# Two projection stages whose later attention outputs are loaded by channel block and split once

## Chip, cores and metric

The kernel runs on one core of a Trainium2 chip. The metric is the device time of one execution in microseconds (us); lower is better. A "TensorE clock" below is the clock that the chip granted, as a share of 2.4 GHz: 1.00 is 2.4 GHz, 0.50 is 1.2 GHz.

## What is computed

Two token groups (prompt and sample), each 1024 tokens by 1024 channels, go through the same two layers. The first layer is attention, the second a pooling mixer.

```python
for l in range(2):
    shift, scl, gate = split(silu(c) @ ada_w[l] + ada_b[l])
    h = rmsnorm(x, pre_norm[l]) * (1 + scl) + shift
    m = attn_mixer(h) if l == 0 else pool_mixer(h)
    x = x + gate * rmsnorm(m, post_norm[l])

def attn_mixer(h):                 # y @ w_out is the "projection" of this study
    qa, ka, va, qb, kb, vb, gate = split(h @ w_in)
    oa = dilated_window_attention(rope(qa), rope(ka), va)           # 8 heads of 64
    ob = grouped_query_attention(axial_rope(rmsnorm(qb, gq)),
                                 axial_rope(rmsnorm(kb, gk)), vb)   # 8 heads, 2 kv heads
    y = concat(oa, ob) * silu(gate)
    return y @ w_out
```

All matrix products are in fp32 accuracy: each operand is split into a rounded part (`hi`, fp32r) and the remainder (`lo`), and three products hi·hi, hi·lo and lo·hi are summed in PSUM.

## The kernel before

The program runs, in this order: prompt attention, prompt projection (stage s = 0), sample attention, sample projection (stage s = 1), sample pooling layer, prompt pooling layer. A planner orders each engine's instructions ahead of time from its own estimate of durations; what it orders, each engine and the DMA queue of SyncE ("SP" in the rows) then run strictly in that order. `keep_in_program_order` (`pin`) keeps an instruction in the order in which the code names it. `issue_after(ins)` keeps the instructions traced under it behind `ins` on the engine of `ins`. Tile pools give out SBUF space; a tile that takes over the space of an older one waits until the older one has been read for the last time.

**A projection stage** (`outproj0`) walks over 8 tiles of 128 tokens. For each tile TensorE sums 8 channel blocks, 6 matmuls of 512 columns each, into one PSUM tile `S` (`out_mm`, L1012 to L1014); there are two `S` tiles, so tile i + 2 may start when tile i has been read. Reading it is ScalarE's square (`square`, L1165) and VectorE's multiplication (L1166); then VectorE adds the row of x (`added`, L1168), and SyncE stores it (`x1o`, L1169). For s = 1 the row is normalised right away (`normed`: ScalarE L250, VectorE L255 and L256) and turned by TensorE (L268) into the next layer's input, two tiles later. For s = 0 the stage makes the sample attention's input from normalised rows kept in DRAM (`h_affine`, L341 to L343).

The left operand y comes from DRAM, where the attention heads stored it as (channel, token). Tiles 0 to 3 were loaded and split during the attention (`out_pre`), and the products of tiles 0 and 1 are almost done when the stage starts. For tiles 4 to 7 the stage loads y tile by tile: two loads of 256 KB for one tile, each 128 partitions by 4 channel blocks by 128 tokens, so in runs of 512 bytes (`load_y`, L1094). The loads of tile i + 2 stand in SyncE's queue in pinned order behind the store of tile i - 1 and the load of row i + 2, which itself waits for a free one of four row buffers. The split of tile i + 1 (ScalarE L1100, VectorE L1101, two of each) is traced in the middle of tile i's matmuls (`split_y`).

**Behind stage s = 0** the sample attention starts with its key and value unit (`unit_KV`): four pairs of 128-token tiles, 48 matmuls of 256 columns each (L416 to L418), copied out by ScalarE, normalised and rotated on VectorE and GpSimd with the table `tb` of k (`b_norm`), split (`hl`, L574 and L575), and turned by TensorE (L437). Then follows the first query unit (`unit_P`), whose weights come from two tiles `raw` and are split by VectorE and GpSimd (L351, L352). The tables of q and k are made by `consts_B` at the start of that attention: three loads (L383, L387), nine VectorE instructions (L388 to L399).

**In the sample pooling layer**, while its third output product (`outp`) runs, `h_affine` makes the prompt layer's input (L341 to L343) between the gate (`gate_ct`, L1257) and the sum `m` (L1320), all on VectorE.

Of the kernel before, what the change touches and what calls it, by code (L numbers as in the profile page):

```python
# [13 lines left out]
P = 128  # L14
D = 1024
# [45 lines left out]
class Trunk:  # L61
# [256 lines left out]
    def h_affine(self, pool, tags, ahead, hT, src, col, gp):  # L318
# [13 lines left out]
        for k in range(KT):  # L332
            if not behind:
                load()
# [45 lines left out]
    def consts_B(self, ap, bp):  # L380
        nc, t = self.nc, self.t
        cs = ap.tile([P, 2, NT, 32], F32, name=self.n("ropB0"), tag="X", bufs=1)
        nc.sync.dma_start(cs, t["k_ropB"])  # L383
        self.ropB = {}
        gt = ap.tile([P, 3, HD], F32, name=self.n("g0"), tag="r2", bufs=2)
        for i, nm in enumerate(("gq", "gk")):
            nc.sync.dma_start(gt[:, i], t[nm].to_broadcast([P, HD]))  # L387
        nc.vector.tensor_scalar_mul(gt[:, 2], gt[:, 0], 0.125)  # L388
        for nm, g in (("gq", gt[:, 2]), ("gk", gt[:, 1])):
            if nm == "gq":  # L390
                tb = bp.tile([P, 2, NT, HD], F32, name=self.n("tb"), tag="s4", bufs=1)
            else:
                tb = ap.tile([P, 2, NT, HD], F32, name=self.n("tb"), tag="P", bufs=3)
            gl = g[:, None, 0:32].to_broadcast([P, NT, 32])
            gh = g[:, None, 32:64].to_broadcast([P, NT, 32])
            nc.vector.tensor_tensor(tb[:, 0, :, 0:32], cs[:, 0], gl, ALU.mult)
            nc.vector.tensor_tensor(tb[:, 0, :, 32:64], cs[:, 0], gh, ALU.mult)
            nc.vector.scalar_tensor_tensor(tb[:, 1, :, 0:32], cs[:, 1], -1.0, gh, op0=ALU.mult, op1=ALU.mult)
            nc.vector.tensor_tensor(tb[:, 1, :, 32:64], cs[:, 1], gl, ALU.mult)  # L399
            self.ropB[nm] = tb  # L400
# [138 lines left out]
    def unit_KV(self, ap, subs, hT, out):  # L539
# [19 lines left out]
        todo = []  # L559
        for pr in range(4):  # L560
# [10 lines left out]
            for h in range(2):  # L571
                hl = ap.tile([P, 2, 4, HD], F32R, name=self.n("hl"), tag="rhl", bufs=2)
                kb = x[:, :, h : h + 1, :].to_broadcast([P, 2, 2, HD])
                nc.vector.tensor_copy(hl[:, :, 0:2, :], kb)  # L574
                nc.vector.tensor_tensor(hl[:, :, 2:4, :], kb, hl[:, :, 0:2, :].bitcast(F32), ALU.subtract)  # L575
                todo.append((pr, h, hl))
            for h in range(2):
# [56 lines left out]
    def layer0(self, s, hT, ap, side, after_proj, open2, run_h, first=None):  # L634
# [4 lines left out]
        if s == 1:  # L639
            self.consts_B(ap, ap)  # L640
# [57 lines left out]
        next(gens[2])  # L698
# [363 lines left out]
    def outproj0(self, s, wo, op, hN, pre):  # L1062
# [4 lines left out]
        yv = self.y_d[s].rearrange("(k p) c -> p k c", p=P)  # L1067
        hq, late = [], []
        y0, yh, xt, jk, hx, ws = {}, {}, {}, {}, {}, []
# [9 lines left out]
        def load(i):  # L1079
            return nc.sync.dma_start(new(i, xt, "xt", 4), xsrc[i])  # L1080

        def new_y(i):
            if i not in yh:
                yh[i] = [tile([P, 2, 4, P], F32R, "yh", 4) for f in range(2)]

        def new_y0(i):
            if i not in y0:
                y0[i] = [tile([P, 4, P], F32, "y0", 4) for f in range(2)]

        def load_y(i):  # L1090
            if 4 <= i < NT:
                new_y0(i)
                for f in range(2):
                    pin(nc.sync.dma_start(y0[i][f], yv[:, 4 * f : 4 * f + 4, i * P : (i + 1) * P]))  # L1094

        def split_y(i):
            if 4 <= i < NT:
                new_y(i)
                for y, z in zip(yh[i], y0[i]):
                    nc.scalar.activation(y[:, 0], z, AF.Copy)  # L1100
                    nc.vector.tensor_tensor(y[:, 1], z, y[:, 0].bitcast(F32), ALU.subtract)  # L1101
# [10 lines left out]
        def new_ws():  # L1112
            ws.extend(tile([P, 2, 256], F32, "ws", 4) for _ in range(4))

        hN_of = perm = g1 = sh1 = None
        if s == 0:
            for i in range(3):
                load(i)
            pg = self.mrow(op, 0, s, 2, "pg")
            new(0, jk, "jk", 2)  # L1120
            hN_of = self.h_affine(op, (("xk", 4),), 4, hN, self.xn_d, self.col[:, 1], ())
            load_k = next(hN_of)
            new_y(4)
            new_y0(4)
            new_ws()
        else:
            new(0, jk, "jk", 2)
            new_y(4)
            new(0, hx, "hx", 2)
            g1, sh1 = (self.row(op, x) for x in ("g1", "sh1"))  # L1130
            new_ws()
            new_y0(4)
# [5 lines left out]
            nc.sync.dma_start(perm, t["k_perm"])  # L1138
            self.mrow(op, 1, s, 1, None, g1)
            self.mrow(op, 1, s, 0, None, sh1)  # L1140
        ks = (0, 1, 1, 2, 1, 2, 1, 0)
        src = t["pwin"][0] if s else t["win"][8]
        for i in range(NT):
            load_y(i + 2)
            if i == 4:
                self.wi = 1
                self.kvw = self.base.tile([P, 2, KT, 256], F32R, name=self.n("w"), tag="w", bufs=1)
                for q in range(4):
                    pin(nc.sync.dma_start(ws[q], src[:, 2 * q : 2 * q + 2, :]))
            if i < 2:  # L1150
                ps = pre[0][i]
            else:
                ps = self.ptile("S")
                for k in range(KT):
                    y, q = (pre[1][i], k) if i < 4 else (yh[i][k // 4], k % 4)
                    self.out_mm(ps, y, q, wo, k, k == 0, k == KT - 1)
                    if k % 2 == 1:
                        run_h(1)
                    if k == 3:
                        split_y(i + 1)  # L1160
            hq += late
            j = new(i, jk, "jk", 2)
# [7 lines left out]
            if i + 3 < NT:  # L1170
                pin(load(i + 3))
# [502 lines left out]
```

## Time and profile before

| | |
|---|---|
| median of 3 runs | 2333.75 us (2332.66 to 2338.61) |
| the profiled execution | 2335.37 us, with a span of 2333.5 us and 1.9 us around it |
| mean granted TensorE clock | 0.965 |
| stage s = 0, tiles 2 to 7 | 822.3 to 902.2 us |
| stage s = 1, tiles 2 to 7 | 1613.6 to 1729.7 us |

The profile is that of one execution. A window row gives, for a stretch of time, each engine's busy time with its number of instructions, then the granted TensorE clock and the DMA engines' share and rate. A wait row says which instruction waited, for whom, for how long in total, how often, and the longest. Matmuls overlap, so busy time of TensorE hides a lower clock: the clock column shows it.

### The profile page before, as it was taken

What the parts mean: (1) busy time and instruction counts of PE and PEld (TensorE: products, weight loads), DVE (VectorE), ACT (ScalarE), POOL (GpSimd) and SP (SyncE); (2) the same over time, 40 slices, a digit from 0 to 9 for tenths busy, and PEclk for the clock granted to TensorE, in tenths of its full rate; (3) what the DMA queues carried; (4) which work ended last, traced back from release to release, by engine and by line L of the source; (5) the groups of instructions that cost most, each with busy time, mean ns of one, the idle gap of its engine ahead of it and who ended that gap; (6) DMA issues with size and microseconds to landing.
All of it is one profiled execution on the core that took longest, in us unless ns stands there. A gap on an engine that the chain in (4) does not pass through costs nothing.

```text
span 2333.5 us, 38514 instructions
## 1 busy us (share of the span) xinstructions
PE 2140.1 (92%) x13777; PEld 1900.1 (81%) x13777; DVE 1572.6 (67%) x3465; ACT 1065.9 (46%) x2435; POOL 979.5 (42%) x1421
## 2 busy tenths in 40 slices
PE   6999899999999788999999999978689999999998
PEld 4987788899999667998897999967467888788887
DVE  8788888777777744778877776784345544874546
ACT  6455555666666421456666666653222112211112
POOL 3676665123543402643311353442024345673452
PEclk8999999999999799999999999989889999999999
DMA  6123343111212453100000221133233223241113
GB/s 254 54 85 116 98 121 100 47 43 52 67 55 60 139 163 116 37 24 27 25 25 28 62 66 57 46 108 116 88 95 95 95 82 126 83 166 41 59 42 148
DMA packets 162784, 193.26 MB, mean 83 GB/s; under 512 B 16184, under 2 KB 126112, under 8 KB 162592
## 3 DMA queue, kind: packets, MB, share of 16 engines
q1 hardware_dynamic: 162288, 190.01, 25.9%
q8 instruction: 109, 1.79, 0.3%
q10 hardware_dynamic: 304, 0.79, 0.1%
q14 instruction: 83, 0.68, 0.1%
HBM read 148.56 MB, written 42.18 MB: 82 GB/s over the span
## 4 chain that ended last, share of the span: by engine, by line
PE 34%; DVE 11%; DMA 6%; ACT 4%; POOL 3%; issue 3%; SPq 0%; POOLq 0%; DVEq 0%; ACTq 0%
PE S L1199 3%; PE S L1200 3%; PE S L1201 3%; DMA y<-y_d 3%; PE J L416 2%; PE J L417 2%; PE J L418 2%; PE S L1296 2%; PE S L1297 2%; PE S L1298 2%; PE H L743 2%; PE T L781 2%; DVE E L761 1%; POOL w L352 1%; DVE w L351 1%
## 5 line engine op out<-in xcount | busy, mean ns | idle before, releaser
L352 POOL TENSOR_TENSOR w<-ws,w 128x256 fp32r<-128x256 f32 (+1 forms) x410 | 387.5, 959 | 314.5 <-DVE w L351 229.8
L416 PE MATMUL J<-w,hT 128*128 128x256 f32 x1664 | 481.8, 290 | 2.8 <-ACT xj L429 2.1
L417 PE MATMUL J<-w,hT 128*128 128x256 f32 x1664 | 478.2, 287 | 3.0 <-POOL w L352 2.8
L418 PE MATMUL J<-w,hT 128*128 128x256 f32 x1664 | 477.0, 287 | 3.6 <-DVE hT L1445 3.4
L416 PEld LDWEIGHTS J<-w,hT 128*128 128x128 f32 x1664 | 318.5, 191 | 7.1 <-ACT xj L429 3.9
L417 PEld LDWEIGHTS J<-w,hT 128*128 128x128 f32 x1664 | 318.5, 191 | 7.1 <-POOL w L352 5.2
L418 PEld LDWEIGHTS J<-w,hT 128*128 128x128 f32 x1664 | 318.0, 191 | 6.3 <-DVE hT L1445 4.1
L761 DVE TENSOR_TENSOR E<-T,E 128x512 fp32r<-128x512 f32 x384 | 261.9, 683 | 83.4 <-ACT E L760 80.8
L760 ACT ACTIVATE E<-T 128x512 fp32r<-128x512 f32 x384 | 226.7, 598 | 198.0 <-PE T L781 70.3
L351 DVE CAST w<-ws 128x256 fp32r<-128x256 f32 (+1 forms) x412 | 181.7, 465 | 152.1 <-PE S L1201 72.0
L750 ACT ACTIVATE P<-H,mx 128x512 f32<-128x512 f32 x256 | 173.9, 686 | 109.3 <-DVE mx L745 92.8
L1199 PE MATMUL S<-hT,w 128*128 128x512 f32 x512 | 200.6, 392 | 3.2 <-DVE sg L1257 2.9
L1200 PE MATMUL S<-hT,w 128*128 128x512 f32 x512 | 200.4, 391 | 0.0
L1201 PE MATMUL S<-hT,w 128*128 128x512 f32 x512 | 200.1, 391 | 0.0
L744 DVE TENSOR_REDUCE mx<-H 128x1 f32<-128x512 f32 x256 | 173.7, 682 | 32.5 <-PE H L743 30.8
L781 PE MATMUL T<-identr,P 128*128 128x128 f32 x1024 | 163.6, 275 | 3.7 <-DVE E L761 3.1
L794 PE MATMUL O<-E,v 128*128 128x256 f32 x512 | 143.9, 303 | 15.2 <-DVE E L761 14.5
L860 ACT ACTIVATE P<-H,nm 128x256 f32<-128x256 f32 x256 | 117.9, 474 | 80.3 <-DVE nm L854 79.8
L793 PE MATMUL O<-E,v 128*128 128x256 f32 x512 | 147.2, 296 | 5.2 <-DVE X L815 2.8
L781 PEld LDWEIGHTS T<-identr,P 128*128 128x128 f32 x1024 | 123.5, 141 | 19.5 <-DVE E L761 2.1
L502 POOL TENSOR_TENSOR hl<-xj,hl 128x256 fp32r<-128x256 f32 x64 | 48.3, 758 | 210.1 <-DVE hl L501 141.7
L125 POOL TENSOR_SCALAR rv<-ss 128x1 f32<-128x1 f32 x64 | 22.1, 345 | 254.7 <-ACT hx L1165 78.7
(271 smaller groups left out, 5255.9 us busy)
## 6 DMA issues: line engine op xcount, KB each, us to landing
ws<-win SPq DMA_DIRECT2D x184, 128.0 KB
ws<-ada_w SPq DMA_DIRECT2D x128, 128.0 KB
ws<-pwin SPq DMA_DIRECT2D x64, 256.0 KB
vb<-v_d SPq DMA_DIRECT2D x64, 144.0 KB
xt<-xp SPq DMA_DIRECT2D x16, 512.0 KB
ada<-ada_w SPq DMA_DIRECT2D x16, 512.0 KB
v_d<-v SPq DMA_DIRECT2D x64, 128.0 KB
wos<-wout SPq DMA_DIRECT2D x32, 256.0 KB
```

What stands on the lines that cost most here:

```text
L351: nc.vector.tensor_copy(hi, src)
L352: (nc.vector if dve_lo else nc.gpsimd).tensor_tensor(lo, src, hi.bitcast(F32), ALU.subtract)
L416: nc.tensor.matmul(ps, hi, w[:, 0, k, :], start=(k == 0), stop=False)
L417: nc.tensor.matmul(ps, hi, w[:, 1, k, :], start=False, stop=False)
L418: nc.tensor.matmul(ps, lo, w[:, 0, k, :], start=False, stop=(k == KT - 1))
L750: nc.scalar.activation(p[:, c * 512 : (c + 1) * 512], ps[c], AF.Exp, bias=mx[:, 2:3], accum_out=stat[h][:, i, c : c + 1])
L760: nc.scalar.activation(ov[0], Tv, AF.Copy)
L761: nc.vector.tensor_tensor(ov[1], Tv, ov[0].bitcast(F32), ALU.subtract)
L781: nc.tensor.transpose(T[:, (2 * e + i) * P : (2 * e + i + 1) * P], Pt[(h, 2 * g + i)][:, (2 * kp + e) * P : (2 * kp + e + 1) * P], self.ident)
L1199: nc.tensor.matmul(ps[:, cs], w[:, 0, k, ws], hT[:, k, 0, cs], start=(k == 0), stop=False)
L1200: nc.tensor.matmul(ps[:, cs], w[:, 0, k, ws], hT[:, k, 1, cs], start=False, stop=False)
L1201: nc.tensor.matmul(ps[:, cs], w[:, 1, k, ws], hT[:, k, 0, cs], start=False, stop=(k == KT - 1))
```

## The change

Five parts.

1. In both stages y of tiles 4 to 7 is loaded by channel block: eight loads of 128 channels by the last 512 tokens (256 KB, runs of 2 KB), four of them ahead of the tile loop, the other four as the four buffers `y0` come free. Each block is split once, 512 columns, into a tile `yk` that stays for the stage. Blocks 0 to 2 (in the order 0, 1, 2, 4, 5, 6, 7, 3) are split behind tile 0's `square` and `added`, three more behind tile 1's, the last two behind tile 2's. The matmuls of tiles 4 to 7 take the blocks in that order.
2. To make room there are three row buffers `xt` in place of four, loaded two tiles ahead, three `xk` in place of four, one `jk` for s = 1, and the staged weights `ws` use the `y0` buffers.
3. For s = 0 the loads of the next attention's table constants are issued in the stage at tile 5, and the tables are made behind the last tile's `added` (`table_B`, `tab_q`).
4. `kvd` lists the last split of k (L575) of each pair in `unit_KV`. With it, the rounding of the `raw` weights in `unit_P` is put behind the first pair's last split of k, and the loading and rounding of the second query unit's weights behind the third pair's.
5. In the sample pooling layer each step of `h_affine` is put behind the gate and the sum `m` of the tile before.

```diff
-    def consts_B(self, ap, bp):
+    def consts_B(self, cs, gt, pin=lambda x: x):
...
+        pin(nc.sync.dma_start(cs, t["k_ropB"]))
...
+            pin(nc.sync.dma_start(gt[:, i], t[nm].to_broadcast([P, HD])))
+
+    def table_B(self, nm, tb):
...
     def unit_KV(self, ap, subs, hT, out):
...
+            self.kvd.append(x_)
...
     def unit_P(self, ap, subs, hT, i, out):
-        w = self.load_block(ap, self.t["win"][9 + i], i == 0, raw=raw, z=2 if raw else 1)
+        with self.tc.issue_after(self.kvd[0].ins) if raw else ExitStack():
+            w = self.load_block(ap, self.t["win"][9 + i], i == 0, raw=raw, z=2 if raw else 1)
...
     def layer0(self, s, hT, ap, side, after_proj, open2, run_h, first=None):
...
         if s == 1:
-            self.consts_B(ap, ap)
+            with self.tc.issue_after(self.last.ins):
+                self.table_B("gk", ap.tile([P, 2, NT, HD], F32, name=self.n("tb"), tag="P", bufs=3))
+                self.tab_q(ap)
...
-        next(gens[2])
+        with self.tc.issue_after(self.kvd[2].ins):
+            next(gens[2])
...
     def outproj0(self, s, wo, op, hN, pre):
...
-    pin(nc.sync.dma_start(y0[i][f], yv[:, 4 * f : 4 * f + 4, i * P : (i + 1) * P]))
+        def load_y(k):
+            if k not in y0:
+                y0[k] = tile([P, 512], F32, "y0", 4)
+            return nc.sync.dma_start(y0[k], self.y_d[s, k * P : (k + 1) * P, 512:])
+
+        def split_y(k, behind):
+            if k not in yk:
+                yk[k] = tile([P, 2, 512], F32R, "yk", 8)
+            with ExitStack() as es:
+                for ins in behind:
+                    es.enter_context(self.tc.issue_after(ins.ins))
+                nc.scalar.activation(yk[k][:, 0], y0[k], AF.Copy)
+                nc.vector.tensor_tensor(yk[k][:, 1], y0[k], yk[k][:, 0].bitcast(F32), ALU.subtract)
...
+        order = (0, 1, 2, 4, 5, 6, 7, 3)
...
+            for k in order[:4]:
+                load_y(k)
...
+        ky = ((0, 1, 2), (3, 4, 5), (6, 7))
...
-            if i + 3 < NT:
-                pin(load(i + 3))
+            if 0 < i < NT - 2:
+                pin(load(i + 2))
...
+            if i < 3:
+                for n in ky[i]:
+                    split_y(order[n], (square, added))
+                    if n + 4 < KT:
+                        load_y(order[n + 4])
...
+            if s == 0 and i == 5:
+                cg = tile([P, D], F32, "xk", 3)
+                self.consts_B(cg[:, 0:512].rearrange("p (a t d) -> p a t d", a=2, t=NT),
+                              cg[:, 512 : 512 + 3 * HD].rearrange("p (a d) -> p a d", a=3), pin)
+            self.last = added
...
     def layer1(self, s, hT, lp, hp, run_h, open_l2):
...
-                outp(prev, False, False, each=lambda i: next(h_of))
+                outp(prev, False, False, each=lambda i: i and h_of.send((self.lastg, self.lastm)))
+                h_of.send((self.lastg, self.lastm))
```

## Rows read from the trace of the kernel before

**Rows 1.** The page's first part: busy time, share and instructions of each engine.
```profile
PE 2140.1 (92%) x13777; PEld 1900.1 (81%) x13777; DVE 1572.6 (67%) x3465; ACT 1065.9 (46%) x2435; POOL 979.5 (42%) x1421
```

**Rows 2.** Windows by stage: engines' busy time, PEclk, DMA share, GB/s.
```profile
822.30:844.40 22.10, 22.04 (x96) 17.93 (x96) 8.64 (x8) 3.06 (x4) 1.30 (x3) 1.00 0.47 167
844.40:902.20 57.80, 47.11 (x193) 37.84 (x194) 28.84 (x30) 15.62 (x22) 7.84 (x10) 0.91 0.46 152
902.20:968.70 66.50, 54.16 (x426) 53.21 (x425) 36.23 (x80) 16.21 (x45) 33.92 (x50) 0.90 0.22 68
1613.60:1638.10 24.50, 24.41 (x112) 19.57 (x112) 9.74 (x9) 4.28 (x8) 3.25 (x6) 1.00 0.28 97
1638.10:1729.70 91.60, 61.55 (x226) 47.30 (x227) 37.44 (x42) 20.67 (x38) 14.77 (x25) 0.80 0.25 77
1972.00:2057.00 85.00, 79.33 (x331) 63.81 (x330) 65.23 (x57) 22.76 (x29) 53.67 (x41) 0.96 0.39 139
```

**Rows 3.** Waits of TensorE from 844 to 969 us.
```profile
PE T L437 <- DVE hl L574: 10.4, 1, 10.4
PE S L1012 <- ACT yh L1100: 9.9, 1, 9.9
PE J L417 <- POOL w L352: 1.9, 2, 1.6
```

**Rows 4.** Waits of TensorE from 1638 to 1730 us.
```profile
PE S L1012 <- DVE jk L1166: 22.9, 4, 7.8
PE T L268 <- DVE hx L256: 7.3, 4, 2.5
```

**Rows 5.** Chain that ended last, in stage s = 1: start, duration, what.
```profile
1614.97 10.79 DMA x_d<-xt
...
1627.16 15.64 DMA y<-y_d
1642.83 0.63 ACT yh L1100
1643.46 1.01 ACT hx L1165 x2
1644.49 1.24 DVE jk L1166
```

**Rows 6.** Timeline of ScalarE and VectorE: the split of y, one half tile.
```profile
853.52 0.63 ACT L1100 ACTIVATE yh<-y 128x512 fp32r<-128x512 f32 x1 [17.77 <-DMA y<-y_d]
854.18 0.69 DVE L1101 TENSOR_TENSOR yh<-y,yh 128x512 fp32r<-128x512 f32 x1 [16.20 <-ACT yh L1100]
```

**Rows 7.** The same chain earlier: a weight load of 256 KB in runs of 2 KB.
```profile
1549.95 4.31 DMA wos<-wout
```

**Rows 8.** Timeline of SyncE's queue as the two stages begin.
```profile
820.79 1.27 SPq L327 DMA_DIRECT2D xk<-xn_d  x3
1599.55 2.04 SPq L244 DMA_DIRECT2D row<-mod_d  x2
```

**Rows 9.** The chain from the end of stage s = 0 to the key unit.
```profile
904.13 9.71 DMA g<-gk
...
914.61 1.29 DVE xt L1168
915.91 10.43 DMA x_d<-xt
...
926.47 2.51 DVE w L351 x4
...
932.05 0.19 POOL rv L125
...
936.34 0.30 DVE hl L574
```

**Rows 10.** Window in which the key unit's matmuls run without a wait.
```profile
912.00:926.00 14.00, 14.00 (x121) 14.00 (x120) 4.16 (x10) 2.41 (x7) 0.00 (x0) 1.00 0.36 113
```

**Rows 11.** Wait of TensorE from 1972 to 2057 us, sample pooling layer.
```profile
PE S L1296 <- DVE m L1320: 3.8, 1, 3.8
```

More of the change, by code (lines that the diff above doesn't have):

```diff
@@ L332, in h_affine @@
         for k in range(KT):
-            if not behind:
+            if ahead:
                 load()
@@ L1079, in load @@
         def load(i):
[L1080 to L1093, printed above, removed]
-                    pin(nc.sync.dma_start(y0[i][f], yv[:, 4 * f : 4 * f + 4, i * P : (i + 1) * P]))
[L1096 to L1101, printed above, removed]
+            return nc.sync.dma_start(new(i, xt, "xt", 3), xsrc[i])
+        def load_y(k):
[10 more added lines that the diff above has]
+                nc.vector.tensor_tensor(yk[k][:, 1], y0[k], yk[k][:, 0].bitcast(F32), ALU.subtract)
         def run_h(c):
@@ L1110, in run_h @@
                         hq.pop(0)
-        def new_ws():
-            ws.extend(tile([P, 2, 256], F32, "ws", 4) for _ in range(4))
+        order = (0, 1, 2, 4, 5, 6, 7, 3)
         hN_of = perm = g1 = sh1 = None
         if s == 0:
+            pg = self.mrow(op, 0, s, 2, "pg")
             for i in range(3):
                 load(i)
-            pg = self.mrow(op, 0, s, 2, "pg")
-            new(0, jk, "jk", 2)
[L1121 to L1125, printed above, removed]
-        else:
-            new(0, jk, "jk", 2)
-            new_y(4)
+            hN_of = self.h_affine(op, (("xk", 3),), 0, hN, self.xn_d, self.col[:, 1], ())
+            load_k = next(hN_of)
+            load_k()
+            for k in order[:4]:
+                load_y(k)
+            new(0, jk, "jk", 2)
+        else:
+            new(0, jk, "jk", 1)
+            for k in order:
+                yk[k] = tile([P, 2, 512], F32R, "yk", 8)
             new(0, hx, "hx", 2)
             g1, sh1 = (self.row(op, x) for x in ("g1", "sh1"))
-            new_ws()
-            new_y0(4)
+            y0[0] = tile([P, 512], F32, "y0", 4)
             load(0)
@@ L1148, in outproj0 @@
                 for q in range(4):
+                    ws.append(tile([P, 2, 256], F32, "y0", 4))
                     pin(nc.sync.dma_start(ws[q], src[:, 2 * q : 2 * q + 2, :]))
@@ L1153, in outproj0 @@
                 ps = self.ptile("S")
-                for k in range(KT):
-                    y, q = (pre[1][i], k) if i < 4 else (yh[i][k // 4], k % 4)
-                    self.out_mm(ps, y, q, wo, k, k == 0, k == KT - 1)
+                for k in range(KT) if i < 4 else order:
+                    if i < 4:
+                        y, q = pre[1][i], k
+                    else:
+                        y, q = yk[k][:, :, (i - 4) * P : (i - 3) * P].rearrange("p e (q c) -> p e q c", q=1), 0
+                    self.out_mm(ps, y, q, wo, k, k == 0, k == (KT - 1 if i < 4 else order[-1]))
                     if k % 2 == 1:
                         run_h(1)
-                    if k == 3:
-                        split_y(i + 1)
             hq += late
-            j = new(i, jk, "jk", 2)
+            j = new(i, jk, "jk", 1 if s else 2)
             h = new(i, hx, "hx", 2) if s else j
@@ L1319, in outp @@
                 else:
[L1320 removed]
+                    self.lastm = nc.vector.tensor_tensor(mi, ps, mi, ALU.add)
                 if last:
@@ L1448, in start @@
             load_x(i, "qT", 4)
-        self.consts_B(ap, ap)
+        self.consts_B(ap.tile([P, 2, NT, 32], F32, name="ropB0", tag="X", bufs=1),
+                      ap.tile([P, 3, HD], F32, name="g0", tag="r2", bufs=2))
+        self.tab_q(ap)
+        self.table_B("gk", ap.tile([P, 2, NT, HD], F32, name=self.n("tb"), tag="P", bufs=3))
         ada = self.ada_first(ap, stage)
```

57 lines of the change are left out of this document (28 added, 29 removed).

## The prediction

> **What bounds the kernel now.** I read the page's busy shares first: TensorE is at 92% [rows 1], so time can only come from stretches in which TensorE waits or runs at half clock. The table of windows finds them: most of the attention and pooling runs near full, but tiles 4 to 7 of each projection stage, the key unit behind the first stage, and one stretch of the sample pooling layer do not [rows 2]. The lists of waits then name who is late [rows 3, 4, 11], and the chain of waits says why [rows 5, 9].
>
> In stage s = 1, tiles 2 and 3 take 24.5 us at clock 1.00 with 112 TensorE instructions (96 matmuls and 16 turns). Tiles 4 to 7 need twice that, and take 91.6 us at a mean clock of 0.80 [rows 2]. Waits explain 22.9 + 7.3 = 30.2 us [rows 4]; the other 12.4 us of the excess of 91.6 - 49.0 = 42.6 us are matmuls at 1.2 GHz after the waits. The wait list blames VectorE's multiplication, but the chain shows the true order: the y load lands after 15.6 us, ScalarE splits it, only then comes the square that stands behind the split in ScalarE's queue, then the multiplication that frees the PSUM tile [rows 5]. So ScalarE is held once per tile by a load that was issued late: it stands behind a row load, which waits for a store that takes 10.8 us to land [rows 5]. Stage s = 0 has the same once: 57.8 us where tiles 2 and 3 took 22.1, so 57.8 - 44.2 = 13.6 us, of them 9.9 us in one wait for the split [rows 2, 3].
>
> Behind stage s = 0 the key unit and first query unit take 66.5 us for 426 TensorE instructions [rows 2]. At the undisturbed pitch of 14.0/121 = 0.116 us [rows 10] these are 49.3 us; 17.2 us are lost, 10.4 of them in one wait for the first split of k [rows 3]. The chain: VectorE waits for the table constant to land (9.7 us), behind it stands the last tile's addition, behind that its store (10.4 us), and the rounding of the raw weights waits for that store and stands ahead of k's normalisation [rows 9].
>
> **The change part by part.** *Loads and splits of y.* Bytes stay (eight loads of 256 KB per stage), and so does the split: eight instructions of 0.63 us on ScalarE and eight of 0.69 us on VectorE, 128x512 as before [rows 6]. No engine time is saved. What moves is when: the first four loads go out before the tile loop, the splits lie in tiles 0 to 2. For s = 1 I put the first loads at 1600 us, where a load behind them in the new queue waited for attention buffers [rows 8]. No row shows such a load; its landing is bounded by 4.3 us, a load of equal size and 2 KB runs [rows 7], and by 15.6 us [rows 5]. I take some 5, since size and runs are those of the nearer row. The first four then land by 1605 (1616 by the other bound), and the splits need tile 0's addition, which ended at 1614.97 [rows 5]. The other four go out as buffers come free, about 1617 to 1626 us, and land by 1642 even at 15.6; the last block is needed at 1638.1 + 7/8 x 12.25 = 1648.8. For s = 0 half of the `y0` space comes free at 820.8 [rows 8], so the first four land by 826 (836), the last by 841 (853); tile 4 begins at 844.4 and wants its seventh block at 852.7. Hidden at 5 us; at 15.6 us some 4 us show. Every later tile finds its y split, so ScalarE's queue holds no load any more.
>
> What is late next? VectorE was busy 9.7 of 24.5 us in tiles 2 and 3 of s = 1 and 8.6 of 22.1 in s = 0 [rows 2]: eight splits add 5.5 us spread over three tiles, which fits. With three row buffers, row i + 2 is loaded when the store of row i - 1 has landed: 10.8 us [rows 5] plus a landing between 4.3 and 15.6 us make at most 26.4 us per three tiles, 8.8 per tile, under TensorE's 11.05 and 12.25 (half of 22.1 and of 24.5 [rows 2]). The pinned table loads at tile 5 hold the queue ahead of tile 6's store until a `xk` is free, a few us of a tile; the ring's slack of 3 x (11.05 - 8.8) = 6.8 us covers it. So TensorE sets the pace. I leave 2 us in s = 1 and 1 us in s = 0 for a group of three splits (3 x 0.63 = 1.9 us [rows 6]) standing ahead of a square. Terms: -42.6 + 2.0 = -40.6, and -13.6 + 1.0 = -12.6.
>
> A rule speaks against this part: the Trainium skill, "DMA: Bandwidth & Descriptors", section Specifications, states 512 B as the smallest transfer that runs at line rate. By it the old 512-byte runs lost nothing and the block loads would land as late as before. The rows stand at 15.6 us against 4.3 us, though the slower load also queued behind a store and a row. By the rule the time would be that of the second rival, 2269 us; by the rows it is 2265.
>
> *Tables and roundings.* The same three loads and nine VectorE instructions move. The constants land during tiles 6 and 7, so the last addition no longer waits 9.7 us, its store goes out at once, and the raw rounding (2.5 us on VectorE [rows 9]) stands behind k's first pair instead of ahead of it. What is late next is k's own chain: last addition some 5 us after the last matmul (square, multiplication, addition as in [rows 5, 9]), nine table instructions, then from `rv` to `hl` 936.34 - 932.05 + 0.3 = 4.6 us [rows 9]; about 13 us in all. TensorE has 192 matmuls x 0.116 = 22 us of key work to run meanwhile, if the planner puts the first turns late enough. Bounds: 0 gained (turns planned early, the chain waited for) to 17.2. I take 12: 17.2 less 2.5 for the first turns and 2.7 for later pairs, which now share VectorE and GpSimd with the raw rounding.
>
> *Pooling layer.* TensorE waits 3.8 us for a sum `m` that stands behind input steps [rows 11], and the window's clock of 0.96 means 0.08 x 85 = 6.8 us at half speed, at most 3.4 us lost [rows 2]. Bounds 0 to 7.2; I take 4. The delayed steps cost nothing while VectorE has 20 free us in this window [rows 2].
>
> *Sum.* -40.6 - 12.6 - 12 - 4 = -69.2 us. The profiled execution took 2335.4 us (2333.5 span and 1.9 around it), so 2266.2; it was 1.6 us above the median, so 2265 as a median.
>
> **The rivals.** *First: k's wait stays.* `issue_after` sets only an earliest place; the planner orders the rest, and its estimate put the first turns too early once already [rows 3]. If neither this nor the pooling part gains, 16 us are missing: 2281 us. For it: VectorE is busy 36 of 66.5 us and GpSimd 34 [rows 2], and rounding now falls between the pairs. Against: the two waits of 9.7 and 10.4 us have nothing left to wait for [rows 9]. Chance 0.14.
>
> *Second: y lands as late as before.* 15.6 us per load, worked out above: 4 us in s = 0, none in s = 1, since y is waited for once per stage and not once per tile: 2269 us. Chance 0.08.
>
> *Third: the row ring.* If store and row load together take over 3 x 12.25 = 36.8 us, each tile is stretched; at 45 us, 15 per tile, six tiles in each stage lose 6 x 3.95 + 6 x 2.75 = 40 us: about 2305. Against: 10.8 + 15.6 is the most that the rows allow, and the engines moved only 97 and 167 GB/s in these tiles [rows 2]. Chance 0.05.
>
> *Fourth, slower: squares behind late splits.* The first three tiles had no y wait; now three groups of splits may stand ahead of a square in ScalarE's queue, each waiting for its loads while PSUM stays full. A tile of TensorE work (mean 11.65 us) hides that much. Six groups (three per stage) lose 6 x (L - 11.65) for a landing L, more than the 69 us gained from L = 23 us on; at 25 us the time is 2265 + 80 = 2345. For it: this is the mechanism seen in [rows 5]. Against: the longest landing there is under 16 us, and the loads start a tile ahead. Chance 0.03.
>
> *Fifth: nothing comes of it,* because what is gained here is given back in the replanned attention: within 7 us of 2334. TensorE stands at 92% [rows 1], so there is slack to lose it in, but nothing else in the attention is touched. Chance 0.03.
>
> **How the numbers follow.** The forecast, both stages at TensorE's pace and most of k's wait gone, has 0.67. Its low end is every ceiling at once, 13.6 + 42.6 + 17.2 + 7.2 = 80.6 us: 2253. The upper end takes in the first two rivals and a mixture, k's wait kept and y landing late, 2281 + 4, with a few us for stalls that I did not see: 2290. Range 2252 to 2290, about 0.85 of the chance. Faster by over 0.3% (7 us, about what a measurement can tell from no change) is every case but the last two: 0.94; within 0.3%: 0.03; slower: 0.03.
>
> **What would show it.** Right: both stages' tiles 4 to 7 take about 45 and 50 us at clock 1.00, ScalarE waits for no y load there, the last addition of s = 0 has no constant ahead of it, and TensorE's wait for `hl` is under 5 us. Wrong: a wait for `S` that leads back to a split or a row load, a clock below 1.00 in the tiles, or waits that reappear between the key unit and the first attention slots. The prediction fails most easily at the planner's place for the first turns.

## The result: 3.2% faster, and the profile after

| | before | after |
|---|---|---|
| median of the runs compared (4 each) | 2333.43 us | 2259.98 us |
| ratio | | 0.9678, 95% interval 0.9662 to 0.9695 |
| profiled execution (span) | 2335.4 us (2333.5) | 2259.7 us (2257.9) |
| TensorE's mean granted clock | 0.965 | 0.980 |

The forecast was 2265 us and "faster". The sum over the profiled execution was -69.2 us; -75.6 came.

The windows of the changed kernel, cut where those of [rows 2] were cut by work: tiles 4 to 7 of the first stage, key and first query unit, tiles 2 and 3 and tiles 4 to 7 of the second stage. Columns: stretch, its length, busy time of TensorE, its weight loads, VectorE, ScalarE, GpSimd, each with its count of instructions, then the granted clock, the DMA share and GB/s.

```profile
844.10:889.20 45.10, 45.10 (x198) 37.00 (x198) 24.82 (x23) 11.73 (x16) 7.45 (x10) 1.00 0.45 160
889.20:947.00 57.80, 53.26 (x425) 51.96 (x424) 37.16 (x80) 16.87 (x46) 33.68 (x50) 0.94 0.26 87
1582.50:1606.80 24.30, 24.30 (x113) 19.86 (x114) 18.50 (x21) 11.91 (x22) 4.66 (x10) 1.00 0.47 159
1606.80:1655.20 48.40, 48.40 (x226) 39.28 (x225) 28.41 (x31) 13.74 (x24) 11.99 (x20) 1.00 0.31 117
```

Where 57.8 and 91.6 us stood in [rows 2], there are now 45.1 and 48.4 us, with TensorE busy throughout at clock 1.00, which is 2.4 GHz. The key and first query unit went from 66.5 to 57.8 us, at clock 0.94.

What TensorE still waits for (total, times, longest, in us): first everything from 844.1 to 947 us, then the three largest from 1655.2 us to the end.

```profile
PE J L421 <- POOL w L352: 2.0, 2, 1.0
PE T L441 <- DVE hl L579: 1.2, 2, 0.8
PE J L421 <- DVE w L352: 0.7, 1, 0.7
PE J L420 <- DVE w L351: 0.5, 1, 0.5
```

```profile
PE S L1310 <- ACT y L1289: 6.1, 1, 6.1
PE S L1213 <- DVE sg L1271: 2.9, 1, 2.9
PE S L268 <- ACT xe L289: 1.8, 1, 1.8
```

Against [rows 3, 4] TensorE's waits for a split of y are gone, tiles 2 to 7 of stage s = 1 keep one wait of 1.5 us for the multiplication, and the 10.4 us for k's split are 1.2. Against [rows 11] the 3.8 us for `m` are gone, but the wait for the split of the gated output (ScalarE, L1289) now takes 6.1 us. In the kernel before that split (there L1275) cost 1.9 us, in the window of [rows 11]:

```profile
PE S L1296 <- ACT y L1275: 1.9, 1, 1.9
```

In what follows the places are told by one table, worked out from the first and last matmul of each stretch of each profile (us; "total" is the median of all its runs). "Stage 0" and "stage 1" are tiles 2 to 7; "key" ends at the first attention slot; "attention" runs from there to tile 2 of stage 1.

| kernel | stage 0 | key | attention | stage 1 | rest | total | ratio to before, interval |
|---|---|---|---|---|---|---|---|
| before | 80.1 | 66.2 | 645.1 | 116.0 | 603.9 | 2333.4 | |
| after | 67.4 | 57.6 | 635.5 | 72.7 | 602.7 | 2260.0 | 0.9678 (0.9662 to 0.9695) |
| y_only | 67.3 | 63.0 | 636.3 | 72.7 | 603.2 | 2269.6 | 0.9722 (0.9708 to 0.9735) |
| no_y | 99.2 | 51.7 | 643.6 | 116.4 | 603.0 | 2333.6 | 0.9992 (0.9983 to 1.0001) |
| short_runs | 67.6 | 56.3 | 637.8 | 72.7 | 601.5 | 2257.6 | 0.9667 (0.9654 to 0.9680) |
| row_ring | 68.8 | 59.5 | 637.3 | 72.7 | 602.7 | 2260.7 | 0.9679 (0.9666 to 0.9693) |
| y_ahead | 75.0 | 69.0 | 644.4 | 92.1 | 601.0 | 2309.3 | 0.9892 (0.9879 to 0.9906) |
| tabs_back | 67.4 | 59.6 | 636.7 | 72.7 | 603.0 | 2258.7 | 0.9679 (0.9666 to 0.9692) |
| no_pins | 66.0 | 60.9 | 635.6 | 72.7 | 603.6 | 2264.8 | 0.9702 (0.9689 to 0.9715) |
| xk4 | 69.5 | 56.7 | 636.8 | 72.7 | 601.8 | 2260.4 | 0.9681 (0.9668 to 0.9694) |
| late_loads | 67.8 | 59.4 | 635.7 | 86.6 | 602.4 | 2271.5 | 0.9727 (0.9711 to 0.9743) |
| k_early | 67.6 | 53.3 | 637.1 | 72.7 | 601.2 | 2253.0 | 0.9647 (0.9632 to 0.9662) |
| k_early_ring | 73.3 | 51.5 | 635.9 | 72.7 | 602.3 | 2257.5 | 0.9670 (0.9655 to 0.9684) |
| first_only | 66.0 | 58.6 | 637.7 | 116.4 | 599.5 | 2299.5 | 0.9858 (0.9840 to 0.9876) |

Tile 2 of stage 0 began between 817.5 and 827.2 us in these profiles, the "rest" took 599.5 to 603.9: a difference of 4 us at one place between two profiles is not read as an effect.

### The profile page after: what moved, and what is told of

It reads as the page before. It is cut to its first block, busy times and chain, and to the rows that moved or that the text cites. A ratio compares the mean times of both kernels' runs of the same rounds, so it can differ in the third digit from the quotient of the medians.

```text
span 2257.9 us, 38531 instructions
## 1 busy us (share of the span) xinstructions
PE 2114.2 (94%) x13777; PEld 1883.1 (83%) x13777; DVE 1570.6 (70%) x3465; ACT 1065.9 (47%) x2435; POOL 973.5 (43%) x1421
## 4 chain that ended last, share of the span: by engine, by line
PE 57%; DVE 20%; POOL 6%; issue 6%; ACT 5%; DMA 5%; SPq 0%; POOLq 0%; DVEq 0%; ACTq 0%
PE J L420 5%; PE J L421 5%; PE J L422 5%; PE S L1213 4%; PE S L1215 4%; PE S L1214 4%; DVE E L771 3%; POOL w L352 3%; PE H L753 3%; DVE w L351 3%; PE S L1022 3%; PE S L1023 3%; DVE mx L754 2%; PE S L1024 2%; PE T L791 2%
## 5 line engine op out<-in xcount | busy, mean ns | idle before, releaser
L352 POOL TENSOR_TENSOR w<-ws,w 128x256 fp32r<-128x256 f32 (+1 forms) x402 | 373.2, 942 | 305.1 <-DVE w L351 232.3
L351 DVE CAST w<-ws 128x256 fp32r<-128x256 f32 (+1 forms) x404 | 181.3, 473 | 142.9 <-PE S L1215 74.4
L804 PE MATMUL O<-E,v 128*128 128x256 f32 x512 | 143.1, 301 | 13.9 <-DVE E L771 13.2
L506 POOL TENSOR_TENSOR hl<-xj,hl 128x256 fp32r<-128x256 f32 x64 | 48.4, 758 | 204.7 <-DVE hl L505 148.6
L753 PE MATMUL H<-kh,qT 128*128 128x512 f32 x256 | 112.6, 440 | 8.2 <-ACT P L760 8.1
```

Source lines behind the costliest of these rows:

```text
L351: nc.vector.tensor_copy(hi, src)
L352: (nc.vector if dve_lo else nc.gpsimd).tensor_tensor(lo, src, hi.bitcast(F32), ALU.subtract)
```

## The experiments

**y_only and no_y: which part pays.** y_only is the changed kernel with the tables made at the start of the attention again and without the pins; no_y is the reverse.

```diff
# y_only
-        with self.tc.issue_after(self.kvd[0].ins) if raw else ExitStack():
...
-        with self.tc.issue_after(self.kvd[2].ins):
...
-                outp(... each=lambda i: i and h_of.send((self.lastg, self.lastm)))
+                outp(... each=lambda i: next(h_of))
...
-            with self.tc.issue_after(self.last.ins):   # layer0: tables
+            self.consts_B(...); self.tab_q(ap); self.table_B("gk", ...)
...
-            if s == 0 and i == 5:                      # the loads of the constants in the stage
...
# no_y: outproj0 of before (y by token tile, xt 4, xk 4), with
+                if i == 5:
+                    cg = tile([P, D], F32, "xk", 4)
+                    self.consts_B(...)
```

> The changed kernel with the tables made at the start of the sample attention again and without the three pinned places: of the change, the y part alone. Theory (the parts add up by place): the two projection stages gain what they gain in the changed kernel, 13.0 and 43.4 us, and the key unit takes its 66 us again, with a wait of about 10 us for the first split of k, since the constant lands late: 2333.4 - 56.4 = 2277 us, or 2268 if the 9.4 us that the sample attention gained go with the y part. Rival (the stages' gain is given back behind them): the earlier end of the first stage only lengthens the wait for the constant and the last row, the key unit grows by the 13 us: 2290 us.

> The kernel before with the constants loaded in the stage, the tables behind the last addition and the three pinned places, but with y loaded and split as before. Theory: the stages take their 57.8 and 91.6 us in tiles 4 to 7 again; the key unit and first query unit gain about as in the changed kernel, 9 us, as the constant lands ahead of the last addition: 2333.4 - 9 - 1 = 2323 us, or 2314 if the sample attention's 9.4 us come from the pinned places. Rival (without the y part the last row is what k waits for): the wait for the constant turns into one for the row, nothing is gained: 2333 us.

y_only has 65.5 us of the 73.5 (2335.1 for before in its comparison): both stages as in the changed kernel, the attention's gain with them. Its key unit waits 5.2 us for the first split of k, half of what was expected. The time of 2269.6 us is that of the theory's second form (2268), in which the attention's gain goes with the y part. no_y took the rival's time, but not in the rival's way: its key unit took 51.7 us, 14.5 less than before and even less than in the changed kernel, but stage 0 took 19 more. ScalarE's waits in stage 0 of no_y (818 to 918 us):

```profile
ACT yh L1110 <- DMA y<-y_d: 68.9, 7, 29.3
ACT jk L1175 <- PE S L1024: 11.2, 1, 11.2
```

In the kernel before the same wait comes to 43.1 us over six splits. SyncE's queue shows why it grew (start, us, instruction): only tile 4's two y loads went out at 832, tile 5's followed a store that stood until 853.35. In the kernel before, all four went out from 836.30 on: in its first stage tile 5's loads stand ahead of tile 2's store (849.86), and only in its second stage behind it.

```profile
832.03 7.00 SPq L1104 DMA_DIRECT2D y<-y_d  x2
853.35 0.56 SPq L1179 DMA_DIRECT2D x_d<-xt  x1
...
861.29 2.06 SPq L1104 DMA_DIRECT2D y<-y_d  x2
```

The store waits for an addition, the addition for work behind the split, the split for y: the late load delays the next load. ScalarE's order differs too: in the kernel before it squares tile 2 at 833.50 and meets the first split behind that (853.52), in no_y the first split (849.06) stands ahead of tile 2's square (849.59). So the plan of the stage changed together with the tables and pins, and no_y does not price them alone; it shows that in this plan the 14.5 us gained behind the stage were lost inside it.

**short_runs: run length or place.** Same places of loads and splits, the old shape. One thing changes with the shape: a load now serves one tile, so tile 4 needs two of them and not all eight.

```diff
-            return nc.sync.dma_start(y0[k], self.y_d[s, k * P : (k + 1) * P, 512:])
...
+            i, f = 4 + k // 2, k % 2
+            return nc.sync.dma_start(y0[k]..., yv[:, 4 * f : 4 * f + 4, i * P : (i + 1) * P])
-        order = (0, 1, 2, 4, 5, 6, 7, 3)
+        order = tuple(range(KT))
...
```

> The changed kernel with each y load of 256 KB as four channel blocks of one token tile (512-byte runs, as before the change) in place of one channel block of four tiles (2 KB runs); the places of the loads and splits are the same. Theory (the early place is what pays, since a load that is waited for once per stage costs nothing): within 3 us of 2260. Rival (the run length pays): the loads land some 15 us after they begin in place of 4 to 12, the splits stand in front of the squares in ScalarE's queue, and each of three groups a stage costs a few us: 2270 us or more, with a clock below 1.00 in the stages.

The theory held: 0.9667 against 0.9678, intervals overlapping. ScalarE waits 6.5 and 6.4 us for y in the two stages, where the changed kernel's block loads cost it 5.5 and 6.8. The landing can be read from the fifth load of stage 0, for whose landing ScalarE waits, first in the changed kernel, then in short_runs (start, us, instruction, idle time before it and what ended it):

```profile
826.85 1.29 SPq L1094 DMA_DIRECT2D y<-y_d  x1
840.52 0.63 ACT L1102 ACTIVATE yk<-y 128x512 fp32r<-128x512 f32 x1 [3.68 <-DMA y<-y_d]
```

```profile
826.52 1.28 SPq L1096 DMA_DIRECT2D y<-y_d  x1
840.12 0.63 ACT L1104 ACTIVATE yk<-y 128x512 fp32r<-128x512 f32 x1 [3.34 <-DMA y<-y_d]
```

That is 13.7 us with runs of 2 KB and 13.6 us with runs of 512 bytes; the fifth load of stage 1 takes 7.8 and 7.4 us (1587.93 to 1595.71, 1588.83 to 1596.23). The 2 KB runs buy nothing measurable here. The rule of the Trainium skill that the prediction set against its own landing ("DMA: Bandwidth & Descriptors", Specifications: from 512 bytes on a transfer runs at line rate) agrees with this run.

**y_ahead and late_loads: the place of the load.** y_ahead is the kernel before with one line moved; late_loads delays the first four block loads of the changed kernel.

```diff
# y_ahead (before)
-            load_y(i + 2)                      # head of tile i
             added = ...
+            load_y(i + 3)
             pin(nc.sync.dma_start(x1o[i], xt[i]))
# late_loads (after)
-            for k in order[:4]:                # ahead of the tile loop
-                load_y(k)
             pin(nc.sync.dma_start(x1o[i], xt[i]))
+            if i == 0:
+                for k in order[:4]:
+                    pin(load_y(k))
```

> The kernel before, with one line moved: the y load of tile i + 3 is issued ahead of tile i's store and of row i + 3's load in SP's queue, where the load of the same tile stood behind that store and the next row load. Shape, split, buffers, tables and places of the splits are those of before. Theory (ScalarE was held because the load stood behind a row load that waits for a store): y lands within 16 us of a place one row load earlier, the waits of the splits go in most tiles, and the stages gain 35 to 56 us together: 2278 to 2298 us. Rival 1 (four tiles' blocks must be there before tile 4, two buffers ahead are not enough): one wait for a split stays per tile, the gain is under 20 us: 2315 us or more. Rival 2 (the row loads, now behind the y loads, come late and take the place): 2325 us or more, with waits for rows on VectorE in both stages. The sample attention's last 8 us, which came with the y part, should be absent if they come from the new buffers and present if they come from the loads' order.

> The changed kernel with the first four y loads of each stage issued behind tile 0's store, in place of ahead of the tile loop; blocks, buffers and the order of the splits stay. Theory (ScalarE's queue held by a y load that lands late is what costs time; where the load is issued decides): the loads land some 15 us behind tile 0's addition, the first three splits hold the square of tile 2, the second three that of tile 3 or 4, the clock falls below 1.00: 5 to 15 us lost in each stage, 2270 to 2290 us. Rival (a block load is waited for once per stage, so a late one is hidden by three tiles of work): 2260 to 2264 us.

y_ahead gained 25 us, between the theory's 35 and the first rival's 20: the move pays 24 us in stage 1, but loads that leave two tiles ahead still come late. Pieces of its chain in stage 1 (start, us, what):

```profile
1632.72 14.52 DMA y<-y_d
1647.27 0.63 ACT yh L1100
1647.90 1.01 ACT hx L1164 x2
1648.93 1.24 DVE jk L1165
```

That is [rows 5] again. The chain holds two such landings in this stage, this one and one of 13.02 us, where that of the kernel before holds four (15.64, 14.47, 16.10 and 15.44 us), one for each of tiles 4 to 7. late_loads lost 13.9 us in stage 1, as the theory said, and 0.4 in stage 0, as the rival said, though ScalarE waited about as long for y in both (22.5 and 21.6 us). The lists of TensorE's waits in the two stages of late_loads, stage 0 to 900 us, then stage 1, tell them apart:

```profile
PE J L421 <- POOL w L352: 2.2, 2, 1.2
PE J L420 <- DVE w L351: 2.0, 1, 2.0
PE S L1022 <- DVE jk L1166: 1.5, 1, 1.5
PE S L1022 <- ACT yk L1102: 0.8, 1, 0.8
```

```profile
PE T L268 <- DVE hx L256: 9.1, 2, 6.4
PE S L1022 <- DVE jk L1166: 1.5, 1, 1.5
```

In stage 1 it is the turn (L268) in TensorE's own queue that waits: it needs the normalised row, which stands behind the square, which stands behind the held split; the clock of tiles 4 to 7 falls to 0.91. Stage 0 has no turns, so a held square touches TensorE only once both `S` tiles are full. This reading rests on the two lists; no run took the turns out of stage 1.

**row_ring and xk4: is the ring of rows what is left in the key unit?** In the changed kernel the store of row 2 was issued at 838.37, row 5's load, which waits for it, at 855.24, and the addition that waited for row 5 began at 872.08: 33.7 us, where the prediction had given the ring 26.4. VectorE's waits between 844 and 901 us:

```profile
DVE xt L1172 <- DMA xt<-xp: 16.8, 5, 5.3
DVE jk L1170 <- ACT jk L1169: 5.6, 2, 3.5
```

```diff
# row_ring
+            o = xt[i] if s else j
-            added = nc.vector.scalar_tensor_tensor(xt[i], j, r, xt[i], ...)
-            pin(nc.sync.dma_start(x1o[i], xt[i]))
+            added = nc.vector.scalar_tensor_tensor(o, j, r, xt[i], ...)
+            pin(nc.sync.dma_start(x1o[i], o))
+            if s == 0 and i + 3 < NT:
+                pin(load(i + 3))
# xk4: row_ring with xt 2 in place of 3, xk 4 in place of 3 in stage 0, rows i + 2,
# two of k's blocks loaded ahead of the loop in place of one
```

> The changed kernel, where in the first stage the addition writes to the buffer of the product, the store goes out from there, and row i + 3 is loaded as soon as row i is added, without waiting for the store. Theory (what is left in the key unit is a ring of three row buffers whose store and load take 32 to 37 us): VectorE waits for no row in tiles 3 to 7 (16.8 us in the changed kernel), the last addition comes some 5 us earlier, the key unit and first query unit go from 57.8 to about 53 us: 2255 us. Rival 1 (the planned place of the first turns holds k): the waits and 57.8 us stay, 2260 us. Rival 2 (the transfers themselves are at their limit, so rows land late anyhow): VectorE still waits 10 us or more for rows, 2260 us.

> The kernel of the row ring run (sum written to the product's buffer, rows loaded without waiting for the store), with two row buffers in the first stage in place of three and four buffers for k's normalised input in place of three. Theory (what holds the key unit is k's last input block, which ScalarE waited for 16.1 us in the row ring run; behind it stand the rounding of the raw weights that TensorE waits for, and the last square): ScalarE waits under 6 us for these blocks, the key unit and first query unit go from 59.5 to about 54 us: 2254 us. Rival 1 (the queue as a whole is what is late): the wait moves to the rows, which have 22 us to come back, and nothing is gained: 2260 us or a few more. Rival 2 (the planned order of the key unit): inputs early, time the same: 2260 us.

The rows came in time, VectorE waited for none of them, and the time stayed: the theory of row_ring fell. ScalarE's waits in row_ring, 815 to 895 us, show the other thing that lands late, and a new one:

```profile
ACT hT L341 <- DMA xk<-xn_d: 16.1, 3, 5.5
ACT yk L1102 <- DMA y<-y_d: 14.7, 2, 13.4
ACT jk L1169 <- PE S L1024: 13.8, 2, 10.0
ACT jk L1169 <- DMA x_d<-jk: 11.9, 3, 6.4
```

`xk`, k's normalised input, holds ScalarE; and the square, which writes to the product's buffer, now waits until the store has left it. xk4 cut the wait for `xk` to 4.0 us and the key unit to 56.7 (its theory had 54), and the wait for stores grew from 11.9 to 36.3 us; VectorE now waits 13.9 us for rows. The first half of its theory holds, its first rival takes the gain.

**tabs_back and no_pins: tables or pins.** Each undoes one of them (edits as in y_only).

> The changed kernel with the rotary constants loaded and the tables made at the start of the sample attention again; the pinned places stay. Theory (the constants' landing, 8 to 10 us ahead of the last addition, was the larger part of the 8.5 us that the tables and the pins gain behind the y part): the key unit grows by 5 to 9 us, 2265 to 2269 us. Rival (the pins are what gain): within 3 us of 2260.

> The changed kernel without the three pinned places (rounding of the raw weights behind k's first pair, the next unit's behind its third, the input steps of the pooling layer); the tables stay in the stage. Theory (the pins gain little, since the raw rounding is 2.5 us of VectorE and TensorE's wait in the pooling layer only moved): key unit and first query unit 57.6 to 60 us, the stretch behind the second stage 602.7 to 604: 2260 to 2263 us. Rival (the pins gain the 8.5 us): 2267 us.

tabs_back is as fast as the changed kernel, as its rival said, yet no_pins does not show the pins as the gain: at 2264.8 us it lies between its two numbers, and its interval overlaps the changed kernel's. From tile 2 of stage 0 to the first slot the changed kernel takes 67.4 + 57.6 = 125.0 us, tabs_back 127.0, no_pins 126.9, y_only 130.3. So either one alone is worth some 2 us at this place, which by the scatter above is not shown; together they are worth 5.3 us there. y_only's 9.6 us as a whole are clear of noise (0.9708 to 0.9735 against 0.9662 to 0.9695); most of the rest lies ahead of tile 2, where the scatter is that large. The part for the pooling layer shows no gain: 603.6 us without it, 602.7 with it, 601.0 in y_ahead, which never had it. In no_pins TensorE waits 3.2 us for `m` and 1.9 us for the split there, 5.1 us in all, where the changed kernel has 6.1 us for the split alone: the wait only moved.

**k_early and k_early_ring: k's input ahead.** All three `xk` buffers are filled ahead of the loop, and each block is used one tile earlier.

```diff
-            load_k()
+            for k in range(3):
+                load_k()
-        kh = ((), (0,), (1,), (2, 3), (4,), (5, 6), (7,), ())
+        kh = ((0,), (1,), (2, 3), (4,), (5, 6), (7,), (), ())
-            for _ in range((2, 1, 1, 2, 1, 0, 0, 0)[i]):
+            for _ in range((1, 1, 2, 1, 0, 0, 0, 0)[i]):
```

> The changed kernel with three of k's input blocks loaded ahead of the first stage's tile loop in place of one, and each block's affine step one tile earlier. Theory (what is left in the key unit comes from k's input blocks, which ScalarE waits for 17.9 us; VectorE's affine step waits with it, and behind that stand the rounding of the raw weights and the last rows): ScalarE's wait for the blocks falls under 8 us, TensorE's waits for w behind the stage go, and key unit with first query unit go from 57.6 to some 53 us: 2255 us. Rival (the row ring holds the last addition at 10 us behind the last matmul): 2260 us.

> k_early and the row ring run's edit together (sum written to the product's buffer, rows loaded without waiting for the store). Theory (blocks and rows both have to be early): 2253 us, last addition within 6 us of the stage's last matmul. Rival 1 (the planned order of the key unit sets its time): inputs early, time of k_early or 2260. Rival 2 (squares now wait for stores that take 10 to 20 us to land): the stage grows by 2 us, 2260 us.

k_early has the lowest time of the study, 0.9647; its interval ends where the changed kernel's begins and overlaps that of short_runs. The key unit takes 53.3 us at clock 1.00, where it took 56.3 to 60.9 in the seven kernels with the y part in this stage, tables or pins or both, and the old places of `xk` (three buffers) (window, columns as above):

```profile
885.10:938.40 53.30, 49.91 (x425) 49.16 (x424) 34.14 (x77) 16.21 (x45) 32.95 (x50) 1.00 0.28 91
```

The mechanism is seen on VectorE around the end of the stage, first in the changed kernel, then in k_early (start, us, instruction, idle time before it and what ended it):

```profile
887.83 1.28 DVE L1172 SCALAR_TENSOR_TENSOR xt<-jk,rr,xt 128x1024 f32<-128x1024 f32 x1 [5.27 <-DMA xt<-xp]
889.99 0.81 DVE L342 TENSOR_SCALAR xk<-xk,col 128x1024 f32<-128x1024 f32 x1 [0.88 <-ACT hT L341]
890.72 0.76 DVE L351 CAST w<-y 128x512 fp32r<-128x512 f32 x2
891.39 2.29 DVE L343 TENSOR_TENSOR hT<-xk,hT 128x1024 fp32r<-128x1024 f32 x1
```

```profile
883.19 1.28 DVE L1173 SCALAR_TENSOR_TENSOR xt<-jk,rr,xt 128x1024 f32<-128x1024 f32 x1 [6.65 <-DMA xt<-xp]
884.40 0.76 DVE L351 CAST w<-y 128x512 fp32r<-128x512 f32 x2
886.30 1.22 DVE L1171 TENSOR_TENSOR jk<-S,row 128x1024 f32<-128x1024 f32 x1 [1.15 <-ACT jk L1170]
```

The last rounding of the key weights (L351, `w<-y`) came at 890.72, behind k's last input block and 1.5 us after TensorE had finished the stage; in k_early at 884.40, before the stage's end at 885.1. In the changed kernel TensorE waits three times for these weights (0.5, 1.0 and 1.0 us, up to 891.29, 892.65 and 894.86), and from 893.2 us, behind the second of these waits, it runs 6.8 us at 1.2 GHz; in k_early it waits 0.3 us there, and the same stretch behind the stage's end runs at 2.4 GHz (windows, columns as above, the changed kernel first):

```profile
893.20:900.00 6.80, 5.81 (x28) 5.52 (x27) 2.02 (x3) 0.00 (x0) 2.35 (x3) 0.50 0.50 157
889.10:895.90 6.80, 6.80 (x60) 6.80 (x59) 1.50 (x2) 0.00 (x0) 0.00 (x0) 1.00 0.47 158
```

Half of the 5.8 us that TensorE is busy at 1.2 GHz is lost to the clock: by this estimate some 3 of the 4.3 us that k_early gains at this place. Of its theory the time came, the conditions in part: TensorE's waits for `w` behind the stage fell from 2.5 to 0.3 us, but ScalarE's wait for the blocks from 17.9 only to 10.8 us, not under 8. The whole kernel gained 7.0 us; what lies beyond the 4.3 us stands ahead of tile 2, within the scatter.

The last addition stays late, 9.3 us behind the last matmul, at clock 1.00 in the key unit: the row ring is no limit that shows in the time. With the ring opened as well (k_early_ring) the key unit takes 51.5 us, but the squares wait 26.8 us for stores and stage 0 grows to 73.3 us, by 5.7 us where the second rival had 2: its mechanism held.

**first_only: where the attention's gain comes from.** The changed kernel, with the function of before for stage 1.

```diff
-        run_h = self.outproj0(s, ...)
+        run_h = (self.outproj0b if s else self.outproj0)(s, ...)   # outproj0b: that of before
```

> The changed kernel with the second projection stage (s = 1) as it was before the change: y loaded and split by token tile, four row buffers, two product buffers. All else is changed. Theory (the sample attention's last 8 us come with the second stage's code, by way of the plan of the attention's last heads, which the stage's first loads and splits share): the first slot of the sample attention begins some 21 us earlier than in the kernel before, this lead stays at 21 to 24 us to the start of the second stage's tile 2, and tiles 2 to 7 take 116 us again: 2333.4 - 22 = 2311 us. Rival (they come with the earlier start of the attention, or with the other parts): the lead grows to some 31 us ahead of tile 2: 2302 us.

The theory fell, and the rival's time (2302 us) is near the 2299.5 us measured: with the old second stage the attention still ends 7 us better than it begins. Its lead over the kernel before, taken at the heads' stores of y, is 25 us from the first head to the eleventh, 27 at the last but one and 32 at the last.

## Why the prediction was right, point by point

- **Stage 1, -40.6:** measured 116.0 - 72.7 = 43.3 us. The full ceiling of 42.6 came; the 2 us set aside for splits ahead of a square did not show. Cause shown: late_loads brings 13.9 us back, y_only has all of it, first_only, with the old second stage, none (116.4 us), and one moved line (y_ahead) has 23.9 us of it. The account of the lateness was incomplete. The prediction put it on "a row load, which waits for a store"; in the kernel before the row loads wait 3.3 us for a store, once, and the stores 42.8 us for the addition behind the split (SyncE's waits, 1560 to 1745 us). So the first late load made the next ones late:

```profile
SPq L1169 <- DVE xt L1168: 42.8, 5, 14.8
SPq L1080 <- DMA x_d<-xt: 3.3, 1, 3.3
```

- **Stage 0, -12.6:** measured 80.1 - 67.4 = 12.7 us, and 12.8 in y_only. Here the place ahead of the loop is not needed: late_loads gives back 0.4 us.
- **The reason given for the landing** was wrong. The prediction took "some 5" us "since size and runs are those of the nearer row". The loads that ScalarE waited for landed in 7.8 to 13.7 us, nearer to the other bound, with runs of either length (short_runs). So the condition of the second rival, "y lands as late as before", came close to true, and its 4 us in stage 0, for which the prediction gives no working, did not show: the last four loads went out from 826.85 to 830.96 us and ScalarE had split them by 844.9, when tile 4, which takes these blocks last, had just begun. A landing of 13.7 us is hidden there as well as one of 5. That rival did not follow from the rule on 512 bytes either. So the term was right for another reason than the one given. The fourth rival's "the longest landing there is under 16 us" was misread by little: the chain of [rows 5] goes on to one of 16.10 us (at 1670.27).
- **Key and first query unit, -12:** measured -8.6, the term that was mis-sized. "What is late next is k's own chain" is the sentence that failed: k's chain costs 1.2 us (the wait for `hl`), as the table load and the 10.4 us wait are indeed gone. Late next were k's input blocks, and behind them the key weights' rounding; k_early takes that away and gains 4.3 us more at that place, most of it by the clock that no longer falls. The last addition came 10.4 us behind the last matmul (899.60), where the prediction had some 5, since it waited for its row. The planner's place for the first turns, named as the point of most danger, was good.
- **Row ring:** "10.8 + 15.6 is the most that the rows allow" was false, 33.7 us were measured; three tiles of 11.05 us are 33.2, so there is no slack left. It cost nothing that shows, as row_ring and k_early say: the square and the product that free `S` stand ahead of the late addition, and those of the next tile come 11 us later.
- **Pooling layer, -4:** not shown, and this step failed: the wait moved. Before, `m` and the split cost 3.8 + 1.9 = 5.7 us, after, the split alone costs 6.1 us, and the difference of 1.2 us in the time lies within the scatter.
- **Not in the sum: the attention, -9.6.** Most of it falls in its last two heads. ScalarE's wait for the first tiles' y there, before (1536 to 1614 us) and after (1512 to 1583):

```profile
ACT yw L1005 <- DMA y<-y_d: 9.0, 6, 4.7
```

```profile
ACT yw L1015 <- DMA y<-y_d: 2.7, 3, 1.7
```

  In the profile before, the last load of output weights stood behind the first two of these y loads, in the profile after ahead of all of them. The wait is 1.9 to 2.5 us in first_only, y_only, short_runs and k_early, which have the gain, and 7.9 and 9.2 us in no_y and y_ahead, which do not. Neither line is touched by the diff. The gain is there in y_only and first_only and absent in no_y and y_ahead, so it comes with the first stage's new code; whether the place of this one load makes it, and by which of the planner's steps, stays open.

By these terms: -12.7 - 8.6 - 43.3 - 1.2 - 9.6 = -75.4, and 0.2 ahead of tile 2. The sum was 6.4 us short: 9.6 us in the attention were not foreseen and 2.8 us in the stages were held back, while 3.4 us of the key unit and 2.8 us of the pooling layer did not come. That the total lies 5 us from the forecast is in part luck: a gain that nobody priced stood in for gains that did not come.

## What to carry to other kernels

A load that an in-order engine waits for is priced by what stands ahead of it in the issuing queue: if that is a store waiting for the very work the load feeds, each delay makes the next, and moving all such loads ahead of the loop is worth more than their shape. Follow the held instruction to the engine that bounds the kernel: the same 22 us of ScalarE's waits cost 14 us where TensorE's own queue held a turn that depended on it, and 0.4 us where only a double-buffered PSUM tile did. And when two parts each seem worth nothing alone, undo them together before calling either idle.

## What was not expected of the hardware

- 512-byte and 2 KB runs of the same 256 KB load gave the same waits (6.5 and 6.4 us against 5.5 and 6.8) and the same landing (13.6 and 13.7 us in stage 0, 7.4 and 7.8 us in stage 1).
- Landing in this one queue varies more than threefold at one size: 256 KB took 4.3 us once [rows 7], 7.8 and 13.7 us in the changed kernel, 14.5 and 13.0 us in y_ahead. A 512 KB row store took 16.9 us (838.37 to 855.24, when the load that waits for it was issued) at 160 GB/s and a DMA share of 0.45.
- TensorE's waits in the key unit sum to 4.4 us in the changed kernel, where the mean granted clock was 0.94 (6.9 of 57.8 us at 1.2 GHz, the rest at 2.4), and to 3.5 us in k_early, where it was 1.00: waits of nearly the same sum went with and without a drop of the clock. In the changed kernel two of them stood close together just ahead of the drop (up to 891.29 and 892.65, the drop at 893.2); in k_early the longest, 1.9 us, stood alone (up to 911.16).
